# Later modulation vectors of a hybrid attention layer: from VectorE sums to strip matmuls on TensorE

## The chip, the cores and the metric

One core of a Trainium2 chip runs the whole kernel. The metric is device time in microseconds (us) of one execution. The engines of a core work side by side, each through its own queue of instructions in order: TensorE (PE) for matmuls, VectorE (DVE), ScalarE (ACT), GpSimd (POOL), and SyncE (SP), whose queue here issues the loads from HBM. Data lies in an on-chip memory of 128 partitions (SBUF); matmuls write into eight PSUM banks.

## The reference, cut to what matters

One layer over 512 latent tokens of width 1024, with 256 context tokens. A condition vector `c` gives six modulation vectors of length 1024:

```
mod = silu(c) @ w_ada + b_ada                      # w_ada: 1024 x 6144
sh1, sc1, gt1, sh2, sc2, gt2 = split(mod, 6)
h = rms_norm(x, g_norm1) * (1 + sc1) + sh1
...                                                # input projection, window attention,
                                                   # bidirectional gated DeltaNet over chunks of 64
x_new = x + gt1 * merge(y_attn, o_dl, dz, ga, gd)
hm = rms_norm(x_new, g_norm2) * (1 + sc2) + sh2
x_new = x_new + gt2 * (relu(hm @ w_mlp1)**2 @ w_mlp2)
```

`sc1` and `sh1` are needed at the start (for the context tokens too, from `c_ctx`). `gt1` is needed after the output projection, `sh2` and `sc2` ahead of the MLP, `gt2` at the end. These last four are the later vectors: 4 x 1024 sums of 1024 products, over 16 MB of weights.

## The kernel before

Activations are kept as columns: a feature is a partition, a token is a place in the row, in eight tiles of 128 features. Matmuls with big weights are made of three passes, high part by high part, high by low, low by high (`mm3`, L288 to L296), where each weight block of 128 x 1024 is loaded by SP (L266), rounded by ScalarE (L271) and its remainder formed by VectorE (L276). A framework schedules the instructions: within an engine the order in the program can differ from the order of the text, and it adds the waits. SBUF space comes from `alloc`, PSUM from `banks`; a freed piece can be given out again, and then the next writer waits for the last reader.

The order of the work from the place on where the change begins:

- The context scan of the DeltaNet ends (`chain_step`, L1156 to L1220: four groups of 64x64 matmuls for each direction, at L1156, L1175, L1195 and L1213, with VectorE and ScalarE steps between them, L1160, L1161, L1181, L1185, L1187, L1206, L1218, L1220). Matmuls that depend on none of this, gate projections in tiles of 128x512 (L1040) and a branch projection (L1086), are put between the dependent ones by `run_fill`.
- Combine stage, two halves (matmuls L885 to L896, VectorE L875), then the IA stage, also two halves: it forms the masked products of queries and keys, with VectorE at L1293 to L1296 and ScalarE at L1302 to L1305.
- Latent scan: eight steps for both directions, each giving control back three times (after L1156, after L1175, and at its end); `FILL[3]` = 8, 7, 3 fill matmuls go there.
- Transposes (L1336, L1341), the branch products, the output projection with the residual (L1387, uses `modT[:, 0]`), the modulation of the MLP's input (L1404, L1427), the MLP in four parts (L1509, L1606 to L1636).

The first two modulation vectors are computed early by `ada` and `columns` (L220 to L259) on PE. `silu(c)` is the stationary operand, spread over 32 columns; the weights, 128 x 256, move through; four such matmuls write to the four strips of 32 partitions of one PSUM bank (L227, L228), and the sum over the 1024 inputs is made by accumulation. Then ScalarE copies the bank (L244), and two tiny matmuls with selector columns of `prm` turn rows into columns (L249).

The later four are computed by `late_mod` (L1100 to L1109). For each block of 128 outputs, 32 in all, SP loads 512 KB of weights (`wada2`, laid out with an output in each partition and its 1024 inputs in the row) into a buffer of its own, and one VectorE instruction multiplies it with `scr` and sums along the row (L1105); `scr` holds `silu(c)` in each partition, loaded as `crow` (L1255) and passed through `silu2` (L1256). One VectorE add a vector brings in the bias (L1108). The blocks are called for in these places: three in each half of the combine stage (L1269) and of the IA stage (L1281), one in each of four scan steps (L1317), two a tile in the first four tiles of the output projection (L1398, up to a count of 24), and eight in the first part of the MLP (L1606).

Of the kernel before, what the change touches and what calls it, by code (L numbers as in the profile page):

```python
# [26 lines left out]
NHALF = 3  # L27
NONES, NWAIT = 30, 8
AHEAD = 2
LATE = 3  # L30
HPAUSE = 2
FPAUSE, CPAUSE = 12, 12
NPL = ()
# [79 lines left out]
def tile_layer(ctx: ExitStack, tc: tile.TileContext, I: dict, out: bass.AP, dbg=None):  # L113
# [55 lines left out]


    cc = cload("cc", [P, KT, 2])
    prm = cload("prm", [P, 188])
    ones = mats.tile([P, P], F32, name="ones")
    V.memset(ones, 1.0)
    epsc = const.tile([P, 1], F32, name="epsc")
# [38 lines left out]
    scond = scb.ap.rearrange("p (k v) -> p k v", k=KT)  # L214
    V.memset(scb.ap, 0.0)
    act(scond[:, :, 0:2], cc, AF.Silu)
    bada1 = const.tile([P, KT], F32, name="bada1")
    V.tensor_scalar(bada1, bada[:, 8:16], 1.0, None, op0=ALU.add)

# [877 lines left out]

    modT = const.tile([P, 4, 8], F32, name="modT")

    def late_mod(grp):  # L1100

        for j in range(8):
            wa = alloc(1024)
            nc.sync.dma_start(out=wa.ap, in_=I["wada2"][grp, j])
            V.scalar_tensor_tensor(wa.ap, wa.ap, 0.5, scr.ap, op0=ALU.mult, op1=ALU.mult, accum_out=modT[:, grp, j:j + 1])  # L1105
            wa.free()
            if j == 7:
                V.tensor_tensor(modT[:, grp], modT[:, grp], bada[:, 16 + 8 * grp:24 + 8 * grp], op=ALU.add)  # L1108
            yield  # L1109

    late = (x for grp in range(4) for x in late_mod(grp))
    late_n = [0]

    def filler():
        yield from br_a()
# [3 lines left out]

    def run_late(n):  # L1120
        for _ in range(n):
            if late_n[0] < 24:
                late_n[0] += 1
                next(late)

    def run_fill(n):
        for _ in range(n):
# [9 lines left out]
    def chain_step(d, step):  # L1137
# [71 lines left out]
        if lat:  # L1209
            for q in (0, 1, 3, 2):  # L1210
                for a in range(2):
                    r = r2[a ^ UP[q]]
                    PE.matmul(z[r2[a ^ ZP[q]], place(q)], IA[d][r, (cl * 4 + q) * CH:(cl * 4 + q + 1) * CH],  # L1213
                              us[r, UPOS[q] * HD:(UPOS[q] + 1) * HD], start=True, stop=True)
            us.free()
            dst = ot_[:, cl * 256:(cl + 1) * 256]
            if step - NCC < NCL // 2:
                V.tensor_tensor(by2(dst), by2(zq), u, op=ALU.add)  # L1218
            else:
                V.tensor_tensor(by2(zq), by2(zq), u, op=ALU.add)  # L1220
                V.tensor_tensor(dst, dst, zq, op=ALU.add)
                A.activation(zq, dst, AF.Square)
                V.tensor_reduce(oss[:, cl], hv(zq), axis=AX.X, op=ALU.add)
            zqb.free()
# [26 lines left out]
        pass  # L1251
    for b in KTM[:1] + VTM[:1] + XA[0]:
        b.free()
    scr = alloc(1024, True)
    nc.sync.dma_start(out=scr.ap, in_=I["crow"][0])  # L1255
    silu2(scr.ap, scr.ap)  # L1256
    XA[1], xa, xr = [], [], []
    for d in range(2):
        XA[1].append(alloc(2048, True))
# [13 lines left out]
    for b in xr:  # L1273
        b.free()

    IA = [alloc(2048, True), alloc(2048, True)]
    ia = [v64(b.ap) for b in IA]
    for g in range(2):
        ms = slice(16 * g, 16 * g + 16)
        es = slice(512 * g, 512 * g + 512)  # L1280
        run_late(LATE)  # L1281
        run_fill(FILL[2] - FPAUSE)
        qq = bank(2)
        qD, qO = blocks(qq)
        for _ in half_products(qq, 1 + g, qT):
            run_fill(FPAUSE)

        pairs_ = lambda ap: (ap[:, :, 0::3], ap[:, :, 1:3])
        m4 = lambda ap: ap.rearrange("p (c q) i -> p c q i", q=4)
        qd2 = strided(qq.ap, (64, 4), (544, 2), (1, HC)), strided(qq[:, HC:], (64, 4), (480, 2), (1, HC))  # L1290
        for d in range(2):
            ed2, ia2 = pairs_(m4(v3(ED[d][:, es]))), pairs_(m4(ia[d][:, ms, :HC]))
            V.tensor_tensor(ia2[0], ed2[0], qd2[0], op=ALU.mult)  # L1293
            for r, r_ in ((slice(0, 64), slice(64, 128)), (slice(64, 128), slice(0, 64))):
                V.tensor_tensor(ia2[1][r_], ed2[1][r], qd2[1][r], op=ALU.mult)
        V.tensor_tensor(v4(EO[:, es]), v4(EO[:, es]), qO, op=ALU.mult)  # L1296
        qq.free()
        eo2 = pairs_(m4(v3(EO[:, es])))
        for a in range(2):
            lo, hi = quad(a, 0), quad(a, 1)  # L1300
            for d in range(2):
                A.activation(ia[d][hi, ms, HC:], ia[d][hi, ms, :HC], AF.Copy)  # L1302
            for n in range(2):
                A.activation(pairs_(m4(ia[0][lo, ms, HC:]))[n], eo2[n][quad(a ^ n, 0)], AF.Copy)
                A.activation(pairs_(m4(ia[1][hi, ms, :HC]))[n], eo2[n][quad(a ^ n, 1)], AF.Copy)  # L1305
            G.memset(ia[0][hi, ms, :HC], 0.0)
            G.memset(ia[1][lo, ms, HC:], 0.0)
    for b in ED + [EO]:
        b.free()
    dump("kT0", kT[0].ap)  # L1310
# [3 lines left out]
    ot = ot_.ap.rearrange("p (c q v) -> p c q v", c=NCL, q=4)  # L1314
    for n, _ in enumerate(steps(range(NCC, NC_))):
        run_fill(FILL[3][n % 3])
        if n % 3 == 1 and n < 3 * NCL // 2:  # L1317
            run_late(1)
    for _ in fill:
        pass  # L1320
    for b in kT + qT + KTM[1:] + VTM[1:] + XA[1] + IA + zb + Sb[0] + Sb[1]:
        b.free()


# [69 lines left out]
    for ct in range(8 - NHALF):  # L1394
        w = wnext()
        acc = bank()
        mm3(acc.ap, w, ys)
        run_late(2)  # L1398
        residual(ct, acc, slice(0, 512))
        acc.free()  # L1400
    run_late(24)
    rx = alloc(512)
    mA = small([P, 8], "mA2", bufs=1)
    V.scalar_tensor_tensor(mA, modT[:, 2], 1.0, g2, op0=ALU.add, op1=ALU.mult)  # L1404
# [182 lines left out]
    for hf in range(4):  # L1587
        act_, xs = [], []
        for f in range(0 if hf else FT):
            if first:  # L1590
                bufs, _, acc = first.pop(0)
            else:
                bufs = [alloc(1024), alloc(1024)]
                w = wload(I["wm1"][f], bufs=bufs)
                acc = bank()
                mm3(acc.ap.rearrange("p (n t) -> p n t", n=2), w, ms)
            r, hl = alloc(1024), alloc(1024)
            A.activation(r[:, :512], acc.ap, AF.Relu)
            acc.free()
            V.tensor_tensor(r[:, 512:], r[:, :512], r[:, :512], op=ALU.mult)  # L1600
            split(r[:, 512:], hl[:, :512], hl[:, 512:])
            for b in bufs + [r]:
                b.free()
            act_.append(hl)
            xs.append((r32(hl[:, :512]), r32(hl[:, 512:])))
            next(late)  # L1606
        if hf == 0:
            xs7 = combos()
            for _ in late:
                pass  # L1610
            scr.free()
            for b in MH[0]:
                b.part(1024, 1024).free()
        w2 = lambda ct: wload(I["wm2"][ct * 4 + hf])
        ps_ = pairs[hf]
        for i, p_ in enumerate(ps_):
            p_.first()
            if i:
                p_.load2()
            if i + 1 < len(ps_):  # L1620
                p_.second()
            if i + 2 < len(ps_):
                ps_[i + 2].load1()
        ws = [w2(0), w2(1)]
        if hf:
            ps_[-1].second()
        accs = [bank(), bank()]
        ks = list(range(FT))
        for cols in (ks[:FT - 2], ks[FT - 2:]):
            for acc, w in zip(accs, ws):  # L1630
                mm3(acc.ap, w, [xs[k] for k in cols], start=(cols[0] == 0), stop=(cols[-1] == FT - 1), ks=cols)
        for ct in range(8):
            if ct > 1:
                accs.append(bank())
# [49 lines left out]
def pack(i):  # L1684
# [11 lines left out]
    ka = wa.reshape(KT, P, 6, KT, P)  # L1696
    w1 = np.stack([ka[:, :, 1], ka[:, :, 0]], 0).transpose(3, 1, 2, 0, 4)
    a["wada1"] = np.ascontiguousarray(w1.reshape(KT, 2, 4, P, 256).transpose(0, 1, 3, 2, 4).reshape(KT, 2, P, 1024))
    a["wada2"] = np.ascontiguousarray(ka[:, :, 2:].transpose(2, 3, 4, 0, 1).reshape(4, 8, P, 1024))
    a["crow"] = np.ascontiguousarray(np.stack([np.broadcast_to(v, (P, D)) for v in (c_, cn)]))  # L1700
    w = i["w_in"][0]
    o = np.cumsum([0, 512, 128, 128, 512, 512, 512, 512, 16, 16, 1024, 1024])
    aq, ak, av, dq, dk, dv, dz, da, db, ga, gd = (w[:, o[n]:o[n + 1]] for n in range(11))
# [13 lines left out]
    prm = np.zeros((P, 188), np.float32)  # L1717
# [18 lines left out]
    prm[:, 145] = -1.0 * (np.arange(P) % CH < HC)  # L1736
    prm[:, 146] = -1.0 * (np.arange(P) % CH >= HC)
    prm[0::32, 184] = prm[1::32, 185] = 1.0
    a["prm"] = prm
    a.update(_constants())  # L1740
    return a
# [16 lines left out]
```

## Time and profile before

| | us |
|---|---|
| three runs | 908.63, 910.72, 912.35 |
| median | 910.72 |
| span of the profiled execution | 909.7 |
| PE busy | 873.9 |
| DVE busy | 652.9 |
| ACT busy | 496.9 |
| DVE busy with the 32 sums (L1105) | 38.8 |

The span runs from the first to the last instruction of one profiled execution, and is somewhat shorter than the time of a run. A group row of the profile has a line of the kernel, an engine, an operation, output and inputs by name, the shape, how often it occurs, busy time in total and the mean in ns of one, then the idle time of the engine just ahead of it and what ended that. A list of waits has what an engine waited for at a line, with microseconds in total, how often, and the longest. A timeline row has start and length in us, then engine, line and operation; an fp32 matmul leaves two records, so "x8" at a line with four strips is one block. The ends of matmuls are modelled, their starts are measured. "issue" is a wait for nothing that the profile shows.

### The profile page before, as it was taken

The numbers are of one execution on the slowest core, as the hardware profiler recorded it, in microseconds if no ns is written. First come the engines' busy times: TensorE is split into PE (matmuls) and PEld (weight loads), VectorE is DVE, ScalarE is ACT, GpSimd is POOL, SyncE is SP. The second block draws the span as 40 slices with busy tenths as digits, with TensorE's granted clock in tenths as the row PEclk, the third lists the DMA queues.
The fourth block names the chain that finished last, engine by engine and source line by source line (L and its number), as shares of the span: only waits on it lengthen the run. The fifth ranks groups of instructions, "written<-read, shape, count | busy, mean of one in ns | idle before, by whom it ended". The sixth has DMA issues, their size and how long they took to land.

```text
span 909.7 us, 18033 instructions
## 1 busy us (share of the span) xinstructions
PE 873.9 (96%) x7564; PEld 721.3 (79%) x7564; DVE 652.9 (72%) x1111; ACT 496.9 (55%) x881; POOL 26.0 (3%) x42
## 2 busy tenths in 40 slices
PE   8999999989999998889999999999999999999998
PEld 6688667867777676656677789888898899889986
DVE  5665799876778999566666968896587567837631
ACT  6368764475768795475654434463265246424520
POOL 0000001010000001100000000000000000000000
PEclk9999999999999999999999999999999999999999
DMA  9824455532311136523143645453412332334031
GB/s 355 312 76 117 94 131 107 113 73 47 57 36 35 59 121 235 182 67 99 49 152 107 241 127 186 155 170 115 139 48 93 116 116 70 116 93 139 1 116 46
DMA packets 31985, 107.13 MB, mean 118 GB/s; under 512 B 4000, under 2 KB 4512, under 8 KB 31904
## 3 DMA queue, kind: packets, MB, share of 16 engines
q1 hardware_dynamic: 29600, 97.59, 32.1%
q0 software_dynamic: 2304, 8.39, 5.8%
q8 instruction: 59, 0.97, 0.4%
q14 instruction: 22, 0.18, 0.1%
HBM read 103.87 MB, written 2.10 MB: 116 GB/s over the span
## 4 chain that ended last, share of the span: by engine, by line
PE 60%; DVE 20%; ACT 11%; DMA 6%; issue 3%; SPq 0%; ACTq 0%; DVEq 0%
PE banks L293 12%; PE banks L294 12%; PE banks L295 12%; PE banks L1509 11%; PE banks L1040 5%; DMA m<-in_wada 3%; ACT m L164 2%; DVE m L865 2%; DVE m L864 2%; DVE m L1105 2%; DVE m L204 2%; DMA m<-in_wm 1%; DVE wl L276 1%; ACT m L928 1%; DVE m L875 1%
## 5 line engine op out<-in xcount | busy, mean ns | idle before, releaser
L293 PE MATMUL banks<-m,wh 128*128 128x512 f32 (+1 forms) x568 | 213.2, 376 | 0.5 <-ACT m L203 0.5
L294 PE MATMUL banks<-m,wh 128*128 128x512 f32 (+1 forms) x568 | 210.7, 371 | 0.3 <-DVE m L204 0.2
L295 PE MATMUL banks<-m,wl 128*128 128x512 f32 (+1 forms) x568 | 209.8, 370 | 0.0
L271 ACT ACTIVATE wh<-wr 128x1024 fp32r<-128x1024 f32 (+1 forms) x92 | 90.6, 987 | 130.5 <-PE banks L294 102.5
L1509 PE MATMUL banks<-m,m 128*128 128x256 f32 x1008 | 123.2, 284 | 0.9 <-ACT m L203 0.6
L1509 PEld LDWEIGHTS banks<-m,m 128*128 128x128 f32 x1008 | 121.9, 192 | 2.4 <-ACT m L203 1.2
L203 ACT ACTIVATE m<-m 128x512 fp32r<-128x512 f32 (+2 forms) x118 | 81.9, 719 | 75.0 <-DVE m L1487 12.0
L293 PEld LDWEIGHTS banks<-m,wh 128*128 128x128 f32 x568 | 107.0, 189 | 19.2 <-ACT m L203 1.0
L294 PEld LDWEIGHTS banks<-m,wh 128*128 128x128 f32 x568 | 107.0, 188 | 18.8 <-DVE m L204 1.2
L295 PEld LDWEIGHTS banks<-m,wl 128*128 128x128 f32 x568 | 106.9, 188 | 18.6 <-issue 0.7
L1040 PE MATMUL banks<-m,wh 128*128 128x512 f32 x320 | 108.2, 409 | 3.5 <-ACT m L164 3.5
L204 DVE TENSOR_TENSOR m<-m,m 128x512 fp32r<-128x512 f32 (+2 forms) x118 | 92.3, 804 | 22.3 <-ACT m L203 14.1
L276 DVE TENSOR_TENSOR wl<-wr,wh 128x1024 fp32r<-128x1024 f32 (+1 forms) x76 | 84.2, 1110 | 14.9 <-ACT wh L271 12.6
L1636 DVE SCALAR_TENSOR_TENSOR m<-banks,modT,m 128x512 f32<-128x512 f32 x32 | 24.0, 750 | 68.6 <-PE banks L295 68.4
L1040 PEld LDWEIGHTS banks<-m,wh 128*128 128x128 f32 x320 | 59.6, 190 | 16.5 <-ACT m L164 4.0
L1040 PE MATMUL banks<-m,wl 128*128 128x512 f32 x160 | 65.5, 410 | 0.0
L1105 DVE SCALAR_TENSOR_TENSOR m<-m,m 128x1024 f32<-128x1024 f32 x32 | 38.8, 1220 | 14.3 <-DMA m<-in_wada 14.2
L293 PE MATMUL banks<-m,m 128*128 128x256 f32 (+1 forms) x136 | 44.9, 344 | 1.4 <-ACT m L300 1.2
L294 PE MATMUL banks<-m,m 128*128 128x256 f32 (+1 forms) x136 | 45.1, 340 | 0.9 <-DVE m L301 0.8
L295 PE MATMUL banks<-m,m 128*128 128x256 f32 (+1 forms) x136 | 44.6, 337 | 0.0
L164 ACT ACTIVATE m<-banks,st 128x512 f32<-128x512 f32 (+1 forms) x32 | 23.5, 738 | 24.7 <-DVE st L570 24.4
L1040 PEld LDWEIGHTS banks<-m,wl 128*128 128x128 f32 x160 | 30.5, 190 | 6.5
(258 smaller groups left out, 1339.5 us busy)
## 6 DMA issues: line engine op xcount, KB each, us to landing
m<-in_wada SPq DMA_DIRECT2D x48, 512.0 KB, 5.3
wr<-in_wm SPq DMA_DIRECT2D x40, 512.0 KB, 3.6
wr<-in_win SPq DMA_DIRECT2D x39, 512.0 KB, 3.7
m<-in_wm SPq DMA_DIRECT2D x24, 512.0 KB, 3.9
wl<-in_win POOLq DMA_DIRECT2D x16, 512.0 KB, 5.6
m<-in_xT SPq DMA_DIRECT2D x8, 512.0 KB, 5.6
wr<-in_wbr SPq DMA_DIRECT2D x16, 256.0 KB, 2.6
wr<-in_wout SPq DMA_DIRECT2D x8, 512.0 KB, 3.8
```

What stands on the lines that cost most here:

```text
L164: r = A.activation(out_, in_, func, **kw)
L203: A.activation(r32(hi), src, AF.Copy)
L204: (eng or V).tensor_tensor(r32(lo), src, hi, op=ALU.subtract)
L271: upper[0] = A.activation(r32(hi), raw, AF.Copy)
L276: V.tensor_tensor(r32(lo), raw, hi, op=ALU.subtract)
L293: PE.matmul(acc, w[0][:, k, :], xhi, start=(start and i == 0), stop=False)
L294: PE.matmul(acc, w[0][:, k, :], xlo, start=False, stop=False)
L295: r = PE.matmul(acc, w[1][:, k, :], xhi, start=False, stop=(stop and i == n - 1))
L1040: PE.matmul(acc.ap, w[x][:, k, :], hx[k][y], start=(k == p == 0), stop=(k == KT - 1 and p == 2))
L1105: V.scalar_tensor_tensor(wa.ap, wa.ap, 0.5, scr.ap, op0=ALU.mult, op1=ALU.mult, accum_out=modT[:, grp, j:j + 1])
L1509: PE.matmul(dst, r32(self.w[w][i][:, k * P:(k + 1) * P]), xs7[x][k][j], start=(n == 0), stop=(n == 11))
L1636: V.scalar_tensor_tensor(xn_[ct], accs[ct].ap, modT[:, 3, ct:ct + 1], xn_[ct], op0=ALU.mult, op1=ALU.add)
```

## The change

The later four vectors are computed on PE like the first two. `scol` is `silu(c)` as columns. For each vector and each block of 128 inputs, four strip matmuls accumulate into one bank; after the eighth block ScalarE copies it, two tiny matmuls turn it into columns, and VectorE adds the bias while it reads PSUM. The host lays `wada2` out with an input in each partition. `scr`, `crow` and its `silu2` are gone. The loads still are 32 of 512 KB, now into three slots of a ring (`LAHEAD` = 2, two blocks ahead of use).

The calls move: the first one (L1254's place) only issues loads, each half of the combine stage calls for four blocks, the IA stage for none, and each of the 24 places in the latent scan for one. None is left for the output projection and the MLP. The buffers of the IA stage are split into halves of 1024, each half taken when its half of the stage begins.

```
-LATE = 3
+LATE = 4
+LAHEAD = 2
...
-    prm = cload("prm", [P, 188])
+    prm = cload("prm", [P, 192])
...
+    scol = const.tile([P, KT], F32, name="scol")
+    A.activation(scol, scond[:, :, 0], AF.Copy)
...
-    def late_mod(grp):
-
-        for j in range(8):
-            wa = alloc(1024)
-            nc.sync.dma_start(out=wa.ap, in_=I["wada2"][grp, j])
-            V.scalar_tensor_tensor(wa.ap, wa.ap, 0.5, scr.ap, op0=ALU.mult, op1=ALU.mult, accum_out=modT[:, grp, j:j + 1])
-            wa.free()
-            if j == 7:
-                V.tensor_tensor(modT[:, grp], modT[:, grp], bada[:, 16 + 8 * grp:24 + 8 * grp], op=ALU.add)
+    def late_mod():
+
+        work = [(grp, k) for grp in range(4) for k in range(KT)]
+        todo, ready = list(work), []
+        ring = alloc(1024 * (LAHEAD + 1), True)
+
+        def load():
+            if todo:
+                i = len(work) - len(todo)
+                wa = ring[:, i % (LAHEAD + 1) * 1024:(i % (LAHEAD + 1) + 1) * 1024]
+                nc.sync.dma_start(out=wa, in_=I["wada2"][todo.pop(0)])
+                ready.append(wa)
+
+        for _ in range(LAHEAD):
+            load()
+        yield
+        for grp, k in work:
+            if k == 0:
+                rp_ = banks.get(512, True)
+            load()
+            wa = ready.pop(0)
+            for g in range(4):
+                PE.matmul(rp_[32 * g:32 * g + 32, :256], scol[:, k:k + 1].broadcast_to([P, 32]), wa[:, g * 256:(g + 1) * 256],
+                          start=(k == 0), stop=(k == KT - 1))
+            if k == KT - 1:
+                rb_ = alloc(256)
+                A.activation(rb_.ap, rp_[:, :256], AF.Copy)
+                rp_.free()
+                mp_ = banks.get(512, True)
+                mp = mp_[:, 0:8].rearrange("p (h g) -> p h g", h=2)
+                for half in range(2):
+                    PE.matmul(mp[:, half, :], rb_[:, half * P:(half + 1) * P], prm[:, 186:190], start=True, stop=True)
+                rb_.free()
+                hg = lambda ap: ap.rearrange("p (g h) -> p h g", h=2)
+                V.tensor_tensor(hg(modT[:, grp]), mp, hg(bada[:, 16 + 8 * grp:24 + 8 * grp]), op=ALU.add)
+                mp_.free()
             yield
+        ring.free()
...
     def run_late(n):
         for _ in range(n):
-            if late_n[0] < 24:
-                late_n[0] += 1
-                next(late)
+            next(late, None)
...
-    scr = alloc(1024, True)
-    nc.sync.dma_start(out=scr.ap, in_=I["crow"][0])
-    silu2(scr.ap, scr.ap)
+    run_late(1)
...
-    IA = [alloc(2048, True), alloc(2048, True)]
-    ia = [v64(b.ap) for b in IA]
+    IA = [[alloc(1024, True) for _ in range(2)] for _ in range(2)]
     for g in range(2):
...
-        run_late(LATE)
+        ia = [v64(IA[d][g].ap) for d in range(2)]
         run_fill(FILL[2] - FPAUSE)
...
     for n, _ in enumerate(steps(range(NCC, NC_))):
         run_fill(FILL[3][n % 3])
-        if n % 3 == 1 and n < 3 * NCL // 2:
-            run_late(1)
+        run_late(1)
     for _ in fill:
         pass
+    for _ in late:
+        pass
...
-        run_late(2)
         residual(ct, acc, slice(0, 512))
...
-    run_late(24)
...
-            next(late)
         if hf == 0:
             xs7 = combos()
-            for _ in late:
-                pass
-            scr.free()
...
-    a["wada2"] = np.ascontiguousarray(ka[:, :, 2:].transpose(2, 3, 4, 0, 1).reshape(4, 8, P, 1024))
-    a["crow"] = np.ascontiguousarray(np.stack([np.broadcast_to(v, (P, D)) for v in (c_, cn)]))
+    a["wada2"] = np.ascontiguousarray(ka[:, :, 2:].transpose(2, 0, 1, 3, 4).reshape(4, KT, P, 1024))
...
+    for g in range(4):
+        prm[32 * g, 186 + g] = 1.0
```

More of the change, by code (lines that the diff above doesn't have):

```diff
@@ L1098, in tile_layer @@
     modT = const.tile([P, 4, 8], F32, name="modT")
-    def late_mod(grp):
-        for j in range(8):
-            wa = alloc(1024)
-            nc.sync.dma_start(out=wa.ap, in_=I["wada2"][grp, j])
-            V.scalar_tensor_tensor(wa.ap, wa.ap, 0.5, scr.ap, op0=ALU.mult, op1=ALU.mult, accum_out=modT[:, grp, j:j + 1])
-            wa.free()
-            if j == 7:
-                V.tensor_tensor(modT[:, grp], modT[:, grp], bada[:, 16 + 8 * grp:24 + 8 * grp], op=ALU.add)
+    def late_mod():
[31 more added lines that the diff above has]
+                mp_.free()
             yield
-    late = (x for grp in range(4) for x in late_mod(grp))
-    late_n = [0]
+        ring.free()
+    late = late_mod()
     def filler():
@@ L1212, in chain_step @@
                     r = r2[a ^ UP[q]]
-                    PE.matmul(z[r2[a ^ ZP[q]], place(q)], IA[d][r, (cl * 4 + q) * CH:(cl * 4 + q + 1) * CH],
+                    PE.matmul(z[r2[a ^ ZP[q]], place(q)], IA[d][cl // 4][r, (cl % 4 * 4 + q) * CH:(cl % 4 * 4 + q + 1) * CH],
                               us[r, UPOS[q] * HD:(UPOS[q] + 1) * HD], start=True, stop=True)
@@ L1291, in tile_layer @@
         for d in range(2):
-            ed2, ia2 = pairs_(m4(v3(ED[d][:, es]))), pairs_(m4(ia[d][:, ms, :HC]))
+            ed2, ia2 = pairs_(m4(v3(ED[d][:, es]))), pairs_(m4(ia[d][:, :, :HC]))
             V.tensor_tensor(ia2[0], ed2[0], qd2[0], op=ALU.mult)
@@ L1301, in tile_layer @@
             for d in range(2):
-                A.activation(ia[d][hi, ms, HC:], ia[d][hi, ms, :HC], AF.Copy)
+                A.activation(ia[d][hi, :, HC:], ia[d][hi, :, :HC], AF.Copy)
             for n in range(2):
[L1304 to L1307, printed above, removed]
+                A.activation(pairs_(m4(ia[0][lo, :, HC:]))[n], eo2[n][quad(a ^ n, 0)], AF.Copy)
+                A.activation(pairs_(m4(ia[1][hi, :, :HC]))[n], eo2[n][quad(a ^ n, 1)], AF.Copy)
+            G.memset(ia[0][hi, :, :HC], 0.0)
+            G.memset(ia[1][lo, :, HC:], 0.0)
     for b in ED + [EO]:
@@ L1316, in tile_layer @@
         run_fill(FILL[3][n % 3])
-        if n % 3 == 1 and n < 3 * NCL // 2:
-            run_late(1)
+        run_late(1)
     for _ in fill:
         pass
-    for b in kT + qT + KTM[1:] + VTM[1:] + XA[1] + IA + zb + Sb[0] + Sb[1]:
+    for _ in late:
+        pass
+    for b in kT + qT + KTM[1:] + VTM[1:] + XA[1] + IA[0] + IA[1] + zb + Sb[0] + Sb[1]:
         b.free()
@@ L1716, in pack @@
     a["wm2"] = np.ascontiguousarray(m2.transpose(3, 0, 2, 1, 4).reshape(32, P, KT, P))
-    prm = np.zeros((P, 188), np.float32)
+    prm = np.zeros((P, 192), np.float32)
     prm[:, 0:48] = cols(i["b_ada"][0])
```

## The prediction

> **What bounds the kernel now.** I read the page's engine totals and chain first, then a table of windows by stage, then the list of what TensorE (PE) waited for, and last what VectorE (DVE) did around the sums that go.
>
> ```profile
> PE 873.9 (96%) x7564; PEld 721.3 (79%) x7564; DVE 652.9 (72%) x1111; ACT 496.9 (55%) x881; POOL 26.0 (3%) x42
> PE 60%; DVE 20%; ACT 11%; DMA 6%; issue 3%; SPq 0%; ACTq 0%; DVEq 0%
> ```
>
> PE is busy for 873.9 of 909.7 us. The chain that ended last passes through other engines for 40% of the span, but at most of those steps PE had other matmuls to run, so the chain overstates what a faster VectorE can give. The stages that the change touches say how much PE can gain there:
>
> ```profile
> 338.00:398.00 60.00, 51.92 (x1040) 40.09 (x1032) 44.88 (x67) 33.91 (x61) 7.83 (x16) 0.97 0.55 186
> 398.00:470.00 72.00, 66.58 (x1319) 46.97 (x1319) 45.73 (x105) 45.94 (x156) 0.46 (x1) 1.00 0.22 69
> 470.00:481.00 11.00, 10.04 (x45) 7.99 (x45) 10.18 (x18) 6.82 (x11) 0.00 (x0) 1.00 0.65 234
> 481.00:600.00 119.00, 117.80 (x659) 102.44 (x658) 92.74 (x151) 51.85 (x83) 0.00 (x0) 1.00 0.50 165
> 600.00:910.00 310.00, 304.75 (x1811) 271.56 (x1809) 195.47 (x273) 128.08 (x165) 0.00 (x0) 1.00 0.30 97
> ```
>
> The columns are the stretch, its length, then busy time (and instructions) of PE, PE's weight loads, VectorE, ScalarE (ACT) and GpSimd (POOL), the clock granted to PE, the DMA share and GB/s. Rows one to four are the combine and IA stages, the latent scan, what follows it, and the branch and output projections with the start of the MLP. PE's idle time in them is 8.1 + 5.4 + 1.0 + 1.2 = 15.7 us. That is the ceiling of what relief of VectorE can return while the sums run; the last row's 5.2 us lies after the last sum but for the stores and the tail. What ended PE's waits between 340 and 480 us, and after 480:
>
> ```profile
> PE banks L1040 <- ACT m L164: 2.9, 2, 2.3
> PE banks L1175 <- DVE m L1161: 2.5, 4, 0.9
> PE banks L896 <- issue: 2.0, 1, 2.0
> PE banks L1195 <- DVE m L1181: 1.7, 2, 1.2
> PE banks L1195 <- ACT m L1187: 1.2, 1, 1.2
> PE banks L895 <- issue: 1.2, 1, 1.2
> PE banks L1156 <- DVE m L1218: 0.4, 2, 0.2
> PE banks L1213 <- DVE m L1206: 0.4, 1, 0.4
> PE banks L1156 <- DVE m L1220: 0.2, 1, 0.2
> ...
> PE banks L1341 <- DVE m L1336: 1.0, 1, 1.0
> PE banks L1509 <- ACT m L203: 0.6, 1, 0.6
> PE banks L293 <- ACT m L203: 0.5, 1, 0.5
> PE banks L293 <- ACT m L300: 0.5, 1, 0.5
> ```
>
> Each row gives microseconds in total, times, and the longest. No row of PE names the sums (L1105) or their loads: they delay PE only through what stands behind them on VectorE.
>
> **The change part by part.** What goes is the 32 sums and the wait for their data:
>
> ```profile
> L1105 DVE SCALAR_TENSOR_TENSOR m<-m,m 128x1024 f32<-128x1024 f32 x32 | 38.8, 1220 | 14.3 <-DMA m<-in_wada 14.2
> DVE m L1105 <- DMA m<-in_wada: 13.5, 10, 4.2
> 428.28 1.23 DVE m L1105 x2
> ```
>
> VectorE loses 38.8 us of work and 14.3 us of standing idle with a sum at the head of its queue. The last row, a step of the chain, shows how that reaches PE: a sum runs from 428.28 to 429.51 in front of L1161, for which L1175 waits. What PE gets back I take from its list of waits: all of L1175 on L1161 (2.5), of L1040 on L164 (2.9; VectorE's wait for a load passes through ScalarE's weight copies to PE), of L1195 on L1187 (1.2), the three small ones (1.0), and L1195 on L1181 (1.7), because in the changed program L1181 stands ahead of the second L875 transpose instead of behind it. That is 9.3 us. The two "issue" rows (3.2 us) name no engine and stay. Of the 2.6 us after the scan I take 1.5, since VectorE has 16 sums fewer there. Together 10.8 us. The bounds are 0 (PE finds the next wait behind each one removed) and 15.7 us (all the idle time).
>
> The 1.7 us wait has a companion:
>
> ```profile
> 340.00:350.00 10.00, 8.32 (x58) 6.29 (x57) 10.00 (x11) 6.13 (x9) 2.07 (x4) 0.83 0.41 143
> ```
>
> With a granted clock of 0.83 over 10 us, 1.7 us of full-speed work were lost right after that wait. If the dip goes with the wait that comes back; if a new wait of PE in that place brings a dip of its own, it does not. I take half, 0.9, with 1.7 and -1.7 as bounds. [...]
>
> What is added on PE is 32 blocks of four strip matmuls, each 128x32 stationary against 128x256 moving in fp32. The first two modulation vectors already use this form (L228), and there are four tiny L249 matmuls of the later kind:
>
> ```profile
> 24.72 0.64 PE L228 MATMUL banks<-m,m 128*32 128x256 f32 x8
> 25.29 0.51 PE L293 MATMUL banks<-m,m 128*128 128x256 f32 x2
> 25.63 0.52 PE L294 MATMUL banks<-m,m 128*128 128x512 f32 x2
> ...
> 41.96 0.28 PE L295 MATMUL banks<-m,m 128*128 128x256 f32 x1
> 42.16 1.07 PE L228 MATMUL banks<-m,m 128*32 128x256 f32 x16
> 43.17 0.50 PE L293 MATMUL banks<-m,m 128*128 128x512 f32 x1
> ...
> 39.99 0.50 PE L249 MATMUL banks<-c_prm,m 128*128 128x2 f32 x4
> 40.35 0.49 PE L295 MATMUL banks<-m,m 128*128 128x512 f32 x1
> ```
>
> Starts count, since the ends are modelled; an fp32 matmul leaves two records, so x8 is one block. One block holds PE from 24.72 to 25.29, 0.57 us. Two in a row take 42.16 to 43.17, 1.01 us, so a further one costs 0.44. Around a lone block the neighbours also stretch: the 256-column pair after it takes 0.34 us (25.29 to 25.63) where two halves of a 0.23 us fill slot (next fence) make 0.23, and the L295 before the double block takes 0.20 where half a slot is 0.12. That makes 0.57 + 0.11 + 0.08 = 0.76 at most. I take 0.57, since some blocks stand in pairs and threes and the others next to 64x64 groups, which change the tile shape anyway. So 32 x 0.57 = 18.2 us, bounds 14.1 and 24.3. [...]
>
> Each of the four groups ends with an ACT copy of 128x256, two L249-like matmuls and an add on VectorE. Four L249 records take 0.36 us between neighbours (39.99 to 40.35), and two fp32 matmuls are four records, so 4 x 0.36 = 1.4; I take 1.7 with their order after the copy, bounds 1.4 and 3.0 (one 0.38 us wait for such a copy at each). Together PE gets 19.9 us more. The small copy of the condition column early on and the add replacing an add cost nothing: they run beside PE, which does not wait for them; uncovered they would be some tenths.
>
> What is moved is the loads. The changed program issues blocks 0 to 2 from SP behind the third weight load, into one ring of three slots, where the kernel now has this:
>
> ```profile
> 338.09 0.33 SPq L1255 DMA_DIRECT2D m<-in_crow  x1
> 338.46 0.42 SPq L1104 DMA_DIRECT2D m<-in_wada  x1
> 344.46 0.33 SPq L266 DMA_DIRECT2D wr<-in_win  x1
> ...
> 343.37 0.46 PE L1195 MATMUL banks<-m,m 64*64 64x64 f32 x16 [0.46 <-DVE m L1181]
> 348.90 0.62 PE L1040 MATMUL banks<-m,wh 128*128 128x512 f32 x2
> 349.59 0.39 PE L1040 MATMUL banks<-m,wh 128*128 128x512 f32 x1
> ...
> 350.00:360.00 10.00, 8.78 (x282) 6.99 (x282) 8.66 (x14) 7.21 (x14) 1.03 (x2) 1.00 0.97 360
> DMA to landing us min/median/max: 3.5/4.6/6.5
> ```
>
> The ring needs three buffers' space at once, and the last reader of what lies there is the context scan's end, the L1195 group at 343.4 (about 342 if the wait before it shrinks). The first load then lands 3.5 us later at 345.5, the others each 1.5 us after (512 KB at the 360 GB/s of the window). On PE 12 fill matmuls follow that L1195 group, 12 x 0.23 = 2.8 us (three take 348.90 to 349.59), and then the twelve matmuls of blocks 0 to 2: PE is there at 344.8 and waits until 348.5 for the third, of which it fills 1.1 with blocks 0 and 1. That is a wait of 2.6 us that the kernel before doesn't have, minus what it lets VectorE and ScalarE catch up (I take 1.6 left). Block 7's load must wait for block 4 and comes behind a weight load: 4.6 us against some 4 us of work between, 0.8. Together 2.4, bounds 0 and 8 (every landing at 6.5). Behind the waiting block on PE stand the combine matmuls and the fill.
>
> In the scan, blocks come three to a step. Eight steps take 72 us, 9 us each, so a slot read by one block has 9 us until the next block in it is due, against a landing of at most 6.5 us, and 20 more loads of 0.52 MB than now make 146 GB/s on top of 69, below 360. I cost them at nothing; without that cover 24 x 0.5 us would be 12. The scan's fill matmuls stay, so the blocks come on top of them; the steps have 5.4 us idle to take in 14.
>
> The sum: 19.9 + 2.4 - 10.8 - 0.9 = +10.6 us. On the profiled execution's 909.7 us of span that is 920.3; its own time lies around 1.0 us above the span if it is the median run (910.72), which I assume (the runs shown reach from 908.63 to 912.35). So about 921 us.
>
> **The rivals.** *The blocks fit into PE's waits (not slower).* At each place where PE stands idle now, a block is ready and fills the time, and cheaply. PE adds 14.1 + 1.4 = 15.5 to 19.9 us and gets back 15.7 and the dip's 1.7; that gives 908.8 to 913.2, about 911. For it: the blocks depend on nothing but a load, and VectorE's relief is large. Against it: 3.2 us of the idle time are "issue", and PE runs its queue in order, so a block fills a wait only where it stands right ahead of it. It decides if the regained time exceeds 15 us.
>
> *The loads come late.* In place of VectorE, PE itself now waits for the loads, in order, with the chain behind it. VectorE met this 10 times with 13.5 us in 340 to 480. With 8 us in the combine stage instead of 2.4, and half of the 10 meetings' mean of 1.35 us in the scan, +5.6 + 6.8 give 933; with only the first, 927. I call it 930. For it: SP's queue holds each load behind weight loads that wait for their buffers. Against: the 9 us of room in the scan.
>
> *VectorE was no limit (slower).* Its waits were hidden, and the waits in the list are fixed by the step's own dependent sequence, so nothing returns: 910.7 + 19.9 + 2.4 = 933. Against: L1161's row above.
>
> *The sums stay, or PE takes no time for strips.* That the change doesn't do what it says is excluded by the instruction order: no 128x1024 sum is left, and the 128 strip matmuls stand on PE.
>
> **How the numbers follow.** Forecast 0.57, fit into waits 0.20, late loads 0.15, no relief 0.08. About the forecast lie 916 to 926: the strips' bounds are -4 and +6, the relief's -5 and +11, the new waits' -2 and +6, not all at once. The low end, 911, leaves out half of the second case (0.10); the high end, 931, leaves out a fourth of the third (0.04) and most of the last (0.06): 0.2 together. A measurement of this kernel tells 0.5%, 4.6 us, from no change. Below 906.2 even the second case does not reach by its own numbers; it takes a gain that I don't see as well, as in the last window: 0.07. Within, 906.2 to 915.3, lie the rest of the second case and a low tail of the forecast, 0.18; slower 0.75.
>
> **What would show it.** Right: PE's busy time up by 15 to 25 us; in the scan's eight steps each some 1 us longer; L1175 no longer waiting for L1161; a wait of PE for in_wada of 1 to 4 us at the first blocks and none in the scan; the stretch after 481 us of the old time nearly as long as before (within 2 us). Wrong: a scan that is not longer (the second case), waits for in_wada in many scan steps (the third), or a gain in the MLP, where I see only tenths to win.

## The result and the profile after

The changed kernel takes 920.44 us (median of four runs, 918.45 to 921.68) against 911.54 us: ratio 1.0101, 95% interval 1.0077 to 1.0125. It is slower by about 9 us, where 921 us was forecast. A later set of runs on another chip gave 1.0094 (1.0074 to 1.0114). All ratios are of fast runs alone: one run of x3_few, at 928.44 us 1.6% above the fastest of its kernel, is not among them.

The page's totals and chain of the changed kernel:

```profile
PE 889.3 (97%) x7836; PEld 725.7 (79%) x7836; DVE 615.2 (67%) x1046; ACT 498.8 (54%) x885; POOL 26.1 (3%) x42
PE 67%; ACT 13%; DVE 12%; DMA 5%; issue 2%; SPq 0%; ACTq 0%; DVEq 0%
```

VectorE lost 37.7 us of work and PE gained 15.4. The chain agrees: VectorE's share fell from 20 to 12%, PE's rose from 60 to 67%. The profiled spans are 909.7 and 916.7 us, 7.0 us apart where the medians are 8.9 apart: the profiled execution of the changed kernel is the fastest of its four runs (918.45 us, granted clock 1.000; the other three have 0.996).

The windows by stage, cut at the same matmuls as before (columns as in the prediction):

```profile
338.00:396.60 58.60, 55.26 (x1092) 40.60 (x1092) 28.26 (x38) 33.68 (x61) 8.31 (x16) 1.00 0.48 164
396.60:476.40 79.80, 77.62 (x1513) 50.54 (x1512) 43.08 (x102) 46.58 (x158) 0.01 (x1) 1.00 0.51 174
476.40:487.20 10.80, 10.71 (x58) 8.13 (x57) 6.42 (x10) 6.05 (x10) 0.00 (x0) 1.00 0.15 50
487.20:606.00 118.80, 117.75 (x658) 102.91 (x657) 85.56 (x134) 56.72 (x91) 0.00 (x0) 1.00 0.39 129
606.00:916.70 310.70, 305.13 (x1811) 271.38 (x1809) 187.67 (x263) 124.89 (x158) 0.00 (x0) 1.00 0.27 92
```

The combine and IA stages are 1.4 us shorter, although eight blocks were put in. The scan is 7.8 us longer, 72.0 to 79.8. The branch loop, the output projection and the MLP are as long as before, within 1.0 us each (600 to the end at 909.7 is 309.7 us before, 310.7 after): the 16 sums that are gone from there gave nothing. PE's idle time in the first three rows fell from 14.5 to 5.6 us. What ended its waits from 338 to 480 us:

```profile
PE banks L1125 <- DMA m<-in_wada: 1.6, 2, 1.1
PE banks L789 <- ACT m L165: 1.3, 1, 1.3
PE banks L1223 <- ACT m L1215: 1.0, 4, 0.3
PE banks L1203 <- DVE m L1189: 0.8, 1, 0.8
PE banks L899 <- issue: 0.2, 1, 0.2
```

L1125 is the strip matmul; L1184, L1203, L1223 and L1241 are the scan's four groups (before: L1156, L1175, L1195, L1213), L1043 is the fill (L1040). The second scan group (L1203) still waits for VectorE, once and for 0.8 us, in the first scan step; before it was four times and 2.5 us. The third (L1223) now waits for ScalarE, 1.0 us in four waits.

### The profile page after: what moved, and what is told of

The parts are those of the page before. It is cut to its first block, busy times and chain, and to the rows that moved or that the text cites. A ratio compares the mean times of both kernels' runs of the same rounds, so it can differ in the third digit from the quotient of the medians.

```text
span 916.7 us, 18495 instructions
## 1 busy us (share of the span) xinstructions
PE 889.3 (97%) x7836; PEld 725.7 (79%) x7836; DVE 615.2 (67%) x1046; ACT 498.8 (54%) x885; POOL 26.1 (3%) x42
## 4 chain that ended last, share of the span: by engine, by line
PE 67%; ACT 13%; DVE 12%; DMA 5%; issue 2%; SPq 0%; ACTq 0%; DVEq 0%
PE banks L296 13%; PE banks L297 13%; PE banks L298 13%; PE banks L1043 9%; PE banks L1533 7%; DMA m<-in_wada 2%; ACT m L165 2%; DVE m L205 2%; ACT m L931 2%; PE banks L1125 1%; ACT wh L274 1%; PE banks L616 1%; DMA m<-in_wm 1%; ACT m L204 1%; DMA wr<-in_wm 1%
## 5 line engine op out<-in xcount | busy, mean ns | idle before, releaser
L1043 PE MATMUL banks<-m,wh 128*128 128x512 f32 x320 | 105.3, 403 | 0.7 <-ACT m L165 0.6
L1043 PEld LDWEIGHTS banks<-m,wh 128*128 128x128 f32 x320 | 58.7, 188 | 14.0 <-ACT m L165 1.1
L1043 PE MATMUL banks<-m,wl 128*128 128x512 f32 x160 | 65.6, 410 | 0.0
L1043 PEld LDWEIGHTS banks<-m,wl 128*128 128x128 f32 x160 | 30.0, 188 | 7.7 <-issue 1.2
L572 DVE TENSOR_REDUCE st<-banks 128x1 f32<-128x640 f32 (+1 forms) x24 | 22.7, 951 | 12.5 <-PE banks L548 10.2
```

What stands on the lines that cost most here:

```text
L572: V.tensor_reduce(st[:, 0, js], svs, axis=AX.X, op=ALU.max)
L1043: PE.matmul(acc.ap, w[x][:, k, :], hx[k][y], start=(k == p == 0), stop=(k == KT - 1 and p == 2))
```

## The experiments

To compare kernels at one place I use the stretch from the same fill matmul near 338 us to the first of the transposes after the scan (L1341 before; its start was 480.73 us), called "the stage". All late work of the changed kernel lies in it. One window of each kernel, in the order before, x2_none, y2_bare, y1_noload, y0_after:

```profile
338.00:480.70 142.70, 128.26 (x2400) 94.78 (x2392) 100.48 (x188) 86.37 (x226) 8.30 (x16) 0.99 0.39 131
```
```profile
338.10:473.90 135.80, 127.53 (x2397) 95.47 (x2390) 76.38 (x145) 86.01 (x224) 8.30 (x16) 0.96 0.19 57
```
```profile
340.40:476.90 136.50, 127.64 (x2397) 95.49 (x2393) 75.49 (x144) 84.72 (x223) 6.22 (x12) 0.96 0.18 53
```
```profile
337.90:484.30 146.40, 142.37 (x2669) 99.06 (x2660) 77.21 (x150) 86.48 (x227) 10.96 (x17) 1.00 0.16 49
```
```profile
337.70:486.00 148.30, 143.17 (x2668) 98.79 (x2660) 77.19 (x150) 86.51 (x227) 8.30 (x16) 1.00 0.50 162
```

The second number is the length, the third PE's busy time, the third from the end the granted clock. What lies ahead of the stage is nearly the same work in all five, yet y2_bare's execution reaches it 2.4 us late: its granted clock is 0.97 over the first 100 us, where the others have 1.00. So single executions differ by 2 us and more outside the stage, and the ratios are of many runs.

**x1_thin: sums without work**

```
-            V.scalar_tensor_tensor(wa.ap, wa.ap, 0.5, scr.ap, ..., accum_out=modT[:, grp, j:j + 1])
+            V.scalar_tensor_tensor(wa[:, :16], wa[:, :16], 0.5, scr[:, :16], ..., accum_out=modT[:, grp, j:j + 1])
```

> The kernel before, with each of the 32 sums cut to 16 of its 1024 columns (the later modulation vectors are then partial sums); loads, their places and VectorE's wait for each load stay. Theory (the sums reach TensorE through VectorE's queue, by their work and by their waits): the work goes, the waits stay, so about half of 10.8 us comes back, 904 to 908 against 911.5. Rival (VectorE was no limit): 910 to 912. Rival (only the wait for the loads hurts, not the work): 910 to 912 here, and all of the gain in x2_none.

Ratio 0.9963 (0.9948 to 0.9979): 3.4 us of 913.3, at the edge of what the theory gives and past both rivals. The waits did not stay as they were, though. VectorE's wait for the loads in the stage grew from 13.5 us to 23.9, and the two "issue" waits of PE are still there:

```profile
DVE m L1105 <- DMA m<-in_wada: 23.9, 15, 4.3
...
PE banks L895 <- issue: 1.8, 1, 1.8
PE banks L896 <- issue: 1.7, 1, 1.7
```

So part of the time that the work gave back went into longer waits, and x1_thin does not price the work alone.

**x2_none: no sums, no loads**

```
-            wa = alloc(1024)
-            nc.sync.dma_start(out=wa.ap, in_=I["wada2"][grp, j])
-            V.scalar_tensor_tensor(...)
-            wa.free()
```

> The kernel before without the 32 sums and without their loads (the later modulation vectors are the bias alone). Theory: all of the relief comes back, 10.8 us: 899 to 903. Rival (VectorE was no limit): 909 to 912. The difference to x1_thin is the price of the waits for the loads.

Ratio 0.9922 (0.9901 to 0.9942), 7.1 us. More comes back than in x1_thin, but less than the 10.8 us that I had worked out. The difference to x1_thin is not the price of VectorE's waits alone: those had grown there, and x2_none also takes the loads themselves away. PE's waits in its stage tell which of my items were wrong (lines are three less than in the kernel before):

```profile
PE banks L1040 <- ACT m L164: 2.5, 1, 2.5
PE banks L1172 <- DVE m L1158: 1.8, 4, 0.5
PE banks L1192 <- DVE m L1178: 1.7, 2, 1.2
PE banks L786 <- DVE m L1293: 0.8, 1, 0.8
...
PE banks L786 <- issue: 0.2, 1, 0.2
```

With no sum in the program, 2.5 of the 2.9 us at L164, 1.8 of the 2.5 us at the second scan group and all 1.7 us at the third are still there. What went are the "issue" rows (3.2 us before, 0.2 here), and the wait of L1195 for L1187. The "issue" rows go with the loads and not with the sums: between 338 and 400 us they are 3.8 us in x1_thin and 3.7 in x3_few, which load `wada2` there with little or no work for VectorE, and none in y1_noload and z1_sums_moved, with no load and two loads there instead of 13 (y2_bare, also with no load, has 0.5 from 337 to 480 us). So some 3 us of this relief come from the missing loads and not from VectorE's missing work. The changed kernel keeps ten loads there and still has only 0.2 us of such waits (0.8 in y0_after); what sets them off stays open. After the stage x2_none needs 905.0 - 473.9 = 431.1 us where the kernel before needs 909.7 - 480.7 = 429.0: the 16 later sums cost nothing that one execution of each can tell.

**x3_few: four of 32 blocks**

```
-            for g in range(4):
+            for g in range(4 if k == KT - 1 else 0):
...
-                          start=(k == 0), stop=(k == KT - 1))
+                          start=True, stop=(k == KT - 1))
```

> The changed kernel with the strip matmuls of the last block of each vector alone: 28 of 32 blocks are left out, all loads, the four closing steps and the places stay. Theory (a block costs TensorE about 0.5 us of its own wherever it stands): 28 x 0.5 to 0.57 = 14 to 16 us less than 920.4, so 904 to 907. Rival (the blocks fit into waits): 916 to 920, since they filled time that would be idle without them.

Ratio 1.0056 (1.0035 to 1.0077), with runs from 913.68 to 920.73 and a profiled span of 912.1. On the 911.5 us of the expectation that is 916.6: it clearly misses the 904 to 907 of the theory and lies in the rival's range. But the edit does more than leave blocks out. Nothing reads a slot any more whose block has no matmuls, so its next load need not wait, and the loads run ahead. Those issued from 338 to 396 us, in x3_few and in y0_after:

```profile
m<-in_wada SPq DMA_DIRECT2D x25, 512.0 KB, 5.4
...
m<-in_wada SPq DMA_DIRECT2D x10, 512.0 KB, 5.5
```

With 25 loads in the place of 10 come the "issue" waits, 2.2 us before L889 and 1.3 before L899. So x3_few gives no price of a block. Its trace shows why a block can be cheaper in the scan than its own time. The third scan group of one step, without a block ahead of it in x3_few, then with one in the changed kernel:

```profile
410.28 1.43 PE L1223 MATMUL banks<-m,m 64*64 64x64 f32 x32
411.64 0.50 PE L1043 MATMUL banks<-m,wl 128*128 128x512 f32 x1
```
```profile
412.10 0.64 PE L1125 MATMUL banks<-m,scol 128*32 128x256 f32 x8
412.67 0.84 PE L1223 MATMUL banks<-m,m 64*64 64x64 f32 x32
413.43 0.50 PE L1043 MATMUL banks<-m,wl 128*128 128x512 f32 x1
```

Counted by starts, the 32 small matmuls take 1.36 us without the block and 0.76 with it. The 0.57 us of the block come back almost whole in this step. The wait stands in no row of PE in this step: its record of the group counts 1.43 us as busy. The list of the weight loads (PEld) has it, 0.8 us in three waits for ScalarE, here from 409.9 to 411.7 us of x3_few:

```profile
PEld banks L1223 <- ACT m L1215: 0.8, 3, 0.4
```

**x4_double: each block twice**

```
-            for g in range(4):
+            for r, g in [(r, g) for r in range(2) for g in range(4)]:
...
-                          start=(k == 0), stop=(k == KT - 1))
+                          start=(k == 0 and r == 0), stop=(k == KT - 1 and r == 1))
```

> The changed kernel with each block's four strip matmuls issued twice in a row (the later vectors are doubled before the bias). Theory: 32 more blocks at the price of a second block in a row, 0.44 us, up to 0.57: +14 to +18, so 934 to 939. Rival (fit into waits): the 5.5 us of TensorE idle time left between 338 and 476 us are filled first, 926 to 931. If late loads set the time, the second copies would cover waits and come out at the same 926 to 931.

Ratio 1.0211 (1.0186 to 1.0236): some 10 us over the changed kernel by the runs, 0.3 us a block, less than the theory's 0.44. Its profiled execution shows 933.5 us, 16 over y0_after's 917.6, 0.5 a block, but it is the slowest of four runs, and y0_after's the second fastest of six. The median of 932.2 us lies between the theory's and the rival's numbers; on the 911.5 us of the expectation it is 930.8, within the rival's.

**y0_after, y1_noload, y2_bare: the late work taken apart on one chip**

y0_after is the changed kernel itself.

> The changed kernel itself, beside the three others on one chip: ratio about 1.010 to the kernel before, +9 us, as measured already.

```
y1_noload
+        G.memset(ring.ap, 0.0)
...
-                nc.sync.dma_start(out=wa, in_=I["wada2"][todo.pop(0)])
+                todo.pop(0)
```

> The changed kernel without the 32 late loads: the ring is set to zero once by GpSimd, the strip matmuls and the closing steps stay (the later vectors are the bias alone). Theory (the loads cost TensorE only the 1.6 us that it waited for them in the combine stage): 1 to 3 us less than y0_after. Rival (the loads, and the weight loads queued behind them on SP, are what is paid): 6 to 10 us less.

```
y2_bare
     def late_mod():
 
-        work = ...                                 # the whole body
+        V.memset(modT, 0.0)
+        yield
```

> The changed kernel without any late work: no loads, no strips, no closing steps; the split IA buffers and the rest of its order stay (the later vectors are zero). Theory: the same as x2_none, ratio 0.992, 7 us under the kernel before. Rival (the split buffers or the other order cost something by themselves): ratio 0.997 or more.

Measured: 1.0094 (1.0074 to 1.0114), 1.0054 (1.0037 to 1.0071), 0.9944 (0.9927 to 0.9961). From bare to strips without loads it is 1.1% (10 us), and 0.4% (3.7 us, between both expectations) for the loads. The five stage windows above say much the same, with less for the loads: 142.7 before, 136.5 with no late work, 146.4 with strips and closing steps, 148.3 with the loads. So 6.2 us come back, 9.9 are paid for the strips and 1.9 for the loads. The split buffers and the other order cost nothing that can be told: y2_bare and x2_none overlap.

Between y2_bare and y1_noload PE's busy time grows by 14.7 us, but its idle time falls from 8.9 to 4.0. And there is a third term, in the clock. Four short windows of y2_bare:

```profile
344.00:348.00 4.00, 2.48 (x37) 1.94 (x37) 4.00 (x6) 2.41 (x4) 0.00 (x0) 0.84 0.03 6
348.00:352.00 4.00, 4.00 (x15) 3.17 (x14) 3.62 (x4) 2.87 (x6) 0.00 (x0) 0.74 0.47 131
388.00:392.00 4.00, 2.99 (x7) 2.41 (x8) 2.88 (x6) 3.13 (x6) 1.03 (x2) 0.50 0.02 4
392.00:396.00 4.00, 4.00 (x13) 3.12 (x13) 0.51 (x2) 3.22 (x8) 0.00 (x0) 0.69 0.00 0
```

Over 4 us, 0.84 and 0.74 are 1.7 us lost, 0.50 and 0.69 are 3.2, less a half microsecond in which PE stood idle anyway. In the profiled executions the kernel before has the first of these dips, y2_bare and x2_none have two, and the changed kernel has none in the stage. Executions of one kernel differ in this (y2_bare's six runs have granted clocks from 0.990 to 0.998), so the mean over the runs tells more: 0.9945 before (17 runs), 0.9927 in y2_bare, 0.9975 in y1_noload, 0.9965 in y0_after (six each). Taken as a share of the mean span, an estimate, that is 5.0, 6.6, 2.3 and 3.2 us lost. By it the strips without loads take some 14 us at full clock, and some 4 come back through the clock. That they keep the clock up by filling PE's waits fits these numbers, but no run takes it apart.

**x5_ahead: the sums with loads two ahead**

```
+        def load():
+            if todo:
+                wa = alloc(1024)
+                nc.sync.dma_start(out=wa.ap, in_=I["wada2"][todo.pop(0)])
+                ready.append(wa)
...
         for grp, j in work:
+            load()
+            wa = ready.pop(0)
             V.scalar_tensor_tensor(wa.ap, wa.ap, 0.5, scr.ap, ...)
```

> The kernel before with its VectorE sums and their places kept, but each load issued two sums ahead of its use (and the IA buffers split as in the change, for space). The reference is computed in full. Theory (VectorE's waits for the loads are worth the 3.7 us between x1_thin and x2_none): ratio about 0.996, 3 to 4 us under the kernel before. Rival (the waits only move, onto SP's queue or onto the sums' work): 1.0 or above.

Ratio 1.0019 (1.0004 to 1.0034), nothing won. VectorE still waits for the loads (its sum is at L1118 there):

```profile
DVE m L1118 <- DMA m<-in_wada: 9.8, 10, 2.7
```

That is 9.8 us in ten waits instead of 13.5: issuing a load earlier in the text did little here, and PE's "issue" waits are 4.6 us. What holds the loads isn't shown. The 3.7 us between x1_thin and x2_none were not the price of VectorE's waits alone.

**z1_sums_moved: no sums in the combine and IA stages**

```
-LATE = 3
+LATE = 0
...
-        if n % 3 == 1 and n < 3 * NCL // 2:
+        if n % 3 == 1:
             run_late(1)
...
     for ct in range(8):
...
+        if ct < 6:
+            run_late(1)
```

> The kernel before with its VectorE sums, but none in the combine and IA stages: one in each of the eight scan steps, six in the branch loop, ten in the output projection, eight in the MLP. The reference is computed in full. Theory (sums hurt only ahead of 481 us, where TensorE waits for VectorE's chain; after it they are hidden): most of the 5 to 7 us of x2_none and y2_bare, ratio 0.994 to 0.997. Rival (a sum costs the same wherever it stands): 0.999 to 1.001. Rival (VectorE becomes the bound in the branch loop and output projection): above 1.002.

Ratio 1.0035 (1.0021 to 1.0049), the third case in kind. Its stage is 140.5 us, 2.2 shorter than before, so the eight sums in the scan with the loads cost some 4 us against y2_bare's 136.5. What was won is lost behind the stage (911.1 - 478.5 = 432.6 us against 429.0). There PE now waits for VectorE in five rows, 5.0 us in all; before, VectorE's rows were 1.5 us (1.0, 0.3 and 0.2):

```profile
PE banks L1511 <- DVE m L204: 1.7, 2, 1.5
PE banks L295 <- DVE wl L276: 1.4, 2, 1.2
PE banks L1511 <- DVE m L1488: 0.8, 1, 0.8
...
```

Moving the sums wins nothing.

**z2_strips_later: 24 blocks moved out of the scan**

```
     for n, _ in enumerate(steps(range(NCC, NC_))):
         run_fill(FILL[3][n % 3])
-        run_late(1)
...
     for ct in range(8):                            # branch loop
+        if ct < 6:
+            run_late(1)
...
         mm3(acc.ap, w, ys)                         # output projection, five tiles
+        run_late(2)
...
+            run_late(1)                            # MLP, first part, eight
```

> The changed kernel with 24 of its 32 strip blocks moved out of the scan: six into the branch loop, ten into the output projection, eight into the MLP's first part; the eight of the combine stage stay. The reference is computed in full. Theory (in the scan a block lies partly in TensorE's waits and keeps the clock up, after it TensorE has no idle time): each of the 24 costs its full 0.57 us there, 13.7 in all, on the scan of y2_bare; with the closing steps and loads 922 to 927, ratio 1.011 to 1.016. Rival (a block costs the 0.3 us net everywhere): 917 to 920, ratio 1.005 to 1.008.

Ratio 1.0161 (1.014 to 1.0181), the upper end of what the theory has. Its stage, the place of one of its blocks in the branch loop, and its span:

```profile
340.40:479.20 138.80, 132.45 (x2465) 95.70 (x2460) 76.61 (x146) 85.41 (x224) 8.30 (x16) 0.99 0.27 93
...
505.96 0.39 PE L298 MATMUL banks<-m,wl 128*128 128x512 f32 x1
506.28 0.64 PE L1125 MATMUL banks<-m,scol 128*32 128x256 f32 x8
506.85 0.50 PE L296 MATMUL banks<-m,wh 128*128 128x512 f32 x1
507.19 0.39 PE L297 MATMUL banks<-m,wh 128*128 128x512 f32 x1
507.42 0.40 PE L298 MATMUL banks<-m,wl 128*128 128x512 f32 x1
...
core 0: 926.4 us, clock 0.994
```

Taking 24 blocks and three closing steps out of the scan shortens the stage by 148.3 - 138.8 = 9.5 us, 0.40 us a block with all that belongs to it. Behind the stage the same work takes (926.4 - 479.2) - (906.3 - 476.9) = 17.8 us more than y2_bare, 0.74 a block (0.65 against y0_after's 431.6 us behind the stage). Among 128x128 matmuls a block costs 0.32 - 0.23 us before it (505.96 to 506.28), its own 0.57, and 0.34 - 0.23 behind it: 0.77 in all. PE has next to no wait there that it could fill: from 490 to 613 us, where most of the 24 blocks stand, it counts as busy for 123.00 of 123.00 us.

**z3_grouped: three blocks in one place of a step**

```
         run_fill(FILL[3][n % 3])
-        run_late(1)
+        if n % 3 == 2:
+            run_late(3)
```

> The changed kernel with the three blocks of a scan step issued together at the step's third place, none at the first and second. The reference is computed in full. Theory (the entry into and out of a strip group is paid once for three blocks): 16 x 0.13 = 2 us less than the changed kernel, ratio 1.007. Rival (the blocks were of use as cover at the two places that they leave, and three loads then fall due at once): 1.010 or above.

Ratio 1.0133 (1.0111 to 1.0155), the rival: though a further block in a row takes 0.44 us (in the kernel before, two take 1.01 us and one 0.57), the kernel gets about 3 us slower than y0_after (the two intervals just touch), and its stage is 150.4 us, 2.1 longer. The three loads that fall due at once, the rival's other reason, show little: PE waits 1.0 us for `wada2` in the stage, against 0.7 in y0_after. So it fits that the blocks, spread over the step's three places, are worth more as cover than the saved entries.

None of the variants that compute everything beats the kernel before.

## Why the prediction was right

The forecast of 921 us was met, and the reason given holds: PE has to do the added matmuls in a stretch where it was busy for 128.3 of 142.7 us in the kernel before, and VectorE's relief doesn't pay for them. That the total came out so near is in part luck: inside the sum two terms of opposite sign were too large, and they largely cancelled.

- *Relief, forecast 10.8 us: too large.* Measured are 7.1 us (x2_none) and 5.1 (y2_bare, 0.56% of 913.2), clock included. The step that failed is giving the waits at L164, L1161 and L1181 to the sums because a sum stood ahead of them on VectorE in places. Without sums, 6.0 of the 7.1 us in those three rows stay. The "issue" rows, which I had left standing, went instead, with the loads; so even the measured relief is not VectorE's alone. The 1.5 us after 481 us did not come: behind the stage x2_none takes 431.1 us without the 16 sums, the kernel before 429.0 with them.
- *Strips and closing steps, forecast 19.9 us, 0.62 a block: near PE's price where PE is full, too large here.* z2_strips_later shows 0.74 a block where nothing is to be filled. In the stage 32 blocks with four closing steps cost 9.9 us net of loads. PE's busy time grows by only 14.7 us, and 4.9 of these come out of idle time. That it isn't 19.9 fits two things the runs show: a block filled a wait inside a group of the scan (0.6 us at L1223 in one step), and the mean clock is higher with the strips (0.9975 in y1_noload against 0.9927 in y2_bare). Their shares aren't shown. So the rival "the blocks fit into PE's waits" was right for a part of it in the scan. It failed as a forecast because about half of the price remains (9.9 of 19.9 us), and because the idle time it counts shrinks anyway when the sums and their loads go (in the stage from 14.4 us in the kernel before to 8.9 in y2_bare).
- *The ceiling of 15.7 us idle time was no ceiling.* Waits between the matmuls of one group were not in it: in x3_few the 32 matmuls at 410.28 us took 0.6 us longer by their starts than in the changed kernel (1.36 against 0.76), and PE's record counts that as busy.
- *The clock, forecast half of 1.7 us:* in the profiled execution the whole dip is gone (1.00 in the changed kernel's stage). Over all runs the estimated loss fell from 5.0 to 3.2 us, by about twice the forecast's 0.9.
- *New waits, forecast 2.4 us:* 1.6 us by the list of waits, 1.9 by the stage windows, 3.7 by the runs, and elsewhere than worked out. The first three loads were issued at 337.52 us, not at 342, so the ring's space was free earlier than I had read; the twelve matmuls of blocks 0 to 2 found their data. It is block 3 that waited:

```profile
337.52 1.28 SPq L1113 DMA_DIRECT2D m<-in_wada  x3
...
344.70 1.50 PE L1125 MATMUL banks<-m,scol 128*32 128x256 f32 x24
350.04 0.64 PE L1125 MATMUL banks<-m,scol 128*32 128x256 f32 x8 [1.12 <-DMA m<-in_wada]
360.60 0.64 PE L1125 MATMUL banks<-m,scol 128*32 128x256 f32 x8 [0.53 <-DMA m<-in_wada]
...
DMA to landing us min/median/max: 3.3/4.4/6.2
```

  The second wait is block 7's, for which 0.8 us had been worked out. In the scan no block waits for its load: the 9 us of room held.
- *The signs named beforehand* came as named but for one: PE's busy time is up by 15.4 us, at the low end of 15 to 25, scan steps are longer by 7.8 / 8 = 1.0 us, and the time behind the stage is unchanged within 2 us in the profiled execution (429.5 us; y0_after's 431.6 is 2.6 over the kernel before). The second scan group, which was to wait for VectorE no longer, still does so once, for 0.8 us.
- *The time above the span, taken as 1.0 us:* in every run that has both it is 1.7 to 1.8 us. With that the same sum would have given 922 us.

## What to carry to other kernels

Here the work that left VectorE was paid at TensorE's price, most of all where TensorE had no idle time. Price such work at the place where it will stand: the same block cost 0.40 us spread through a scan of dependent steps and 0.74 us among big matmuls. Before counting a wait as regained, take the suspected work out and look whether the wait goes; "it stood ahead of it in the queue" gave 6 us to the sums that were not theirs. When several small edits of opposite sign make up a forecast, a right total says little of the terms. And look at what else an edit sets free: leaving out matmuls also let the loads run ahead (25 instead of 10 from 338 to 396 us), and leaving out work made VectorE's waits for them longer (23.9 us instead of 13.5).

## What the runs showed of the hardware

In the profiled execution of the kernel before, the granted clock fell after short waits of TensorE: 1.2 and 0.5 us, 1.7 of the 4 us from 340 on, then a clock of 0.59 from 344 to 348 us, where six fill matmuls start 0.43 us apart (345.26 to 347.82) instead of 0.23 (348.90 to 350.28), a dip that cost 1.7 us. How long PE stood idle in such a stretch does not tell it alone. The same execution idled for 2.0 of the 4 us from 368 on and kept its clock:

```profile
368.00:372.00 4.00, 1.98 (x68) 1.64 (x59) 2.57 (x6) 1.14 (x2) 0.23 (x1) 1.00 0.27 105
```

Without the late work the clock was lower: y2_bare, with 271 matmul records fewer in the stage than y0_after, has two such dips, at 344 to 352 and 388 to 396 us, and over six runs each a mean clock of 0.9927 against 0.9965. What sets a dip off is not shown.
